# An encoder layer's embedding product moved from among the experts to a place ahead of the gates

## The chip, the cores and the metric

One Trainium2 chip, one core of it. The time is device microseconds of one execution of the whole program; lower is better. PE is the matrix engine, DVE the vector engine, ACT the scalar engine, POOL the general one, and SP issues most of the transfers (DMA). "PEclk" in a view is the clock that was granted to PE, as a share of full speed.

## The reference, cut to what matters

512 tokens of 1024 channels, two layers (`DEPTH = 2`), all in float32.

```python
for i in range(DEPTH):
    h = rmsnorm(x, norm_mix[i])
    proj = h @ w_in[i]
    na_q, na_k, na_v, q_lat, kv_lat, k_rope, gate_a, gate_b = jnp.split(proj, IN_CUTS, axis=-1)
    y_a = neighbourhood_attention(na_q, na_k, na_v, na_rpb[i]) @ w_na_o[i]      # 8 heads, window 8 x 16
    y_b = latent_attention(q_lat, kv_lat, k_rope, ...) @ w_mla_o[i]              # 8 heads
    merged = jax.nn.sigmoid(gate_a) * y_a + jax.nn.sigmoid(gate_b) * y_b
    x = x + merged @ w_out[i]
    x = x + expert_choice_moe(rmsnorm(x, norm_moe[i]), ...)   # 16 experts of 64 tokens each, FF 1024
    ple_gate = jax.nn.sigmoid(rmsnorm(x, norm_ple[i]) @ ple_gate_w[i])
    x = x + ple_gate * (p[i] @ ple_w[i])                      # p: 512 x 256, ple_w: 256 x 1024
return rmsnorm(x, norm_final)
```

The product `p[i] @ ple_w[i]` needs nothing that the layer computes. It is used only at the layer's end.

## The kernel before

All is written in one function, `trunk`, in program order; a scheduler then fixes the order of the instructions on each engine when the program is built, and on the chip each engine keeps to that order and waits where an operand or a buffer isn't ready. A tile of a pool is a buffer: the scheduler makes the next user of the same memory wait until the last user of the old tile is done, and pools that are opened on one side of the memory lie on top of one another like a stack, so a pool opened after another was closed lies on the memory of the closed one.

A layer has these stages:

- **Projections and latent attention.** Weights come through `load_w`: one transfer into `raw` (2 buffers), a copy `wh` on ACT and a rest `wl` on DVE (3 buffers each). A product in higher precision (`mm3`) is three PE products: high by high, high by low, low by high.
- **Neighbourhood attention** (L450 to L487). 8 heads of 4 column blocks, so 32 units a layer. A unit runs through the engines in turn: scores `s` on PE (two products, L462 and L463; 2 buffers in PSUM), bias and maximum on DVE (`sb`, L466; 3 buffers), exponential on ACT (L469), reciprocal on DVE (L471), scaling into one of four padded tiles `pad0` to `pad3` on POOL (L473), two or three transposes `tp` on PE (L477; 2 buffers), a copy `pt` on DVE or ACT (L479). Each two heads end with eight products `o` on PE (L485) and `put_y` on ACT and DVE.
- **Gates and branch outputs** (L494 to L521). For both branches and four column groups: two gate products `tp_` of 24 PE products each (`t_proj`) and two output products `op` of 12 each; the gates' sigmoids go to tiles `sg` of the pool `mp`. That is 8 times 72 products.
- **Output projection** `xo`, norm and router.
- **Experts.** Experts 0 to 3 are gathered one by one (`gather_one`) and computed whole; experts 4 to 9 are gathered together (`gather`, "gather A"), experts 10 to 15 too ("gather B", `GATHER_B = 7`). `hidden` makes the two first products `t` of an expert, whose weights come in tiles of 1 MiB (`w_tile`) into a ring of 15 slots of the pool `s8` (tag `s8`), so long as a slot is free. The outputs of experts 0 to 3 wait in one slot (`obs`) until `scatter` adds them to x, after `hidden` of expert 7. After `hidden` of expert 11 (`PLE_AT = 11`) stands the embedding's product `pw`: `load_s` takes six slots of the ring for p and the weights, 48 PE products follow through one PSUM buffer, and ACT copies the result to two tiles `pw` of a pool of its own.
- **Second products of experts 4 to 15** (`po`, L900), scatter (`sca`), the embedding's gate `pg`, and the end of the layer, where `pw` is used (L968).

Of the kernel before, what the change touches and what calls it, by code (L numbers as in the profile page):

```python
# [10 lines left out]
F32 = mybir.dt.float32  # L11
# [8 lines left out]
P = 128  # L20
D = 1024
S = 512
# [6 lines left out]
RING = 15  # L29
BLOCKED = 4  # L30
EARLY_END = ONE * 8 + BLOCKED * 4 - 4
GATHER_B = 7

PLE_AT = 11
SPL = 3
GTB = 1
S0B = 2
# [26 lines left out]
def trunk(ctx, tc, a, out, L=2, dbg=None):  # L64
# [12 lines left out]
    def slot(dt=F32, shape=(P, 4, S)):  # L77
        return s8.tile(list(shape), dt, tag="s8", name="s8")
# [15 lines left out]
    def acopy(o, i, scale=1.0):  # L94
        sc.activation(o, i, AF.Copy, scale=scale)  # L95
# [48 lines left out]
    def mm3(ps, pairs):  # L144

        n = 3 * len(pairs)
        i = 0
        for (sh, sl), (mh, ml) in pairs:
            for s_, m_ in ((sh, mh), (sh, ml), (sl, mh)):
                pe.matmul(ps, s_, m_, start=(i == 0), stop=(i == n - 1))  # L150
                i += 1
# [30 lines left out]
    for l in range(L):  # L182
# [258 lines left out]
        for c, ps in enumerate(wide([a["w_v"][l, i] for i in range(4)], hT_h, hT_l, "vp")[0]):  # L441
            acopy(v[:, c, :], ps)
        ya_h, ya_l = slot(F32R), slot(F32R)
        mt = ExitStack()
        mp = mt.enter_context(tc.tile_pool(name=f"m{l}", bufs=3, side="right", reuse_waits="tile"))
        with tc.tile_pool(name=f"na{l}", bufs=2, side="right", reuse_waits="tile") as ap_:
            pad = [ap_.tile([P, NCH[c] * P], F32, tag=f"pad{c}", bufs=1, name=f"pad{c}") for c in range(4)]
            for b in pad:
# [40 lines left out]
        if dbg and l == 0:  # L489
            dma(dbg["ya"].rearrange("(k p) t -> p k t", p=P), ya_h.bitcast(F32))  # L490


        tb = [slot() for _ in range(2)]
        m_h = [slot(F32R) for _ in range(2)]  # L494
# [81 lines left out]
                    nw[1] = d  # L576
            return t

        before = [kp.tile([P, 2, S], BF16, tag="row", bufs=3, name="before") for _ in range(2)]
        for i in range(2):  # L580
            sc.dma_start(before[i], a["before"][:, 2 * i:2 * i + 2, :])
        s4_ = small.tile([P, 4], F32, tag="s4_", name="s4_")
# [69 lines left out]
            pe.transpose(aT[:NE, c * P:(c + 1) * P], aff[:, c, :], ident)  # L652

        def row():
            return kp.tile([NE, S], F32, tag="row", bufs=3, name="row")


        cur = row()
# [1 line left out]
        for _ in range(CAP // 8):  # L660
# [2 lines left out]
            nxt = row()  # L663
            ve.match_replace(nxt, m8, cur, -1.0)
            cur = nxt
        sel = row()
        ve.tensor_scalar(sel, cur, 0.0, None, ALU.is_lt)
        cs = row()
        ve.tensor_tensor_scan(cs, sel, sel, 0.0, ALU.add, ALU.max)
        ps1 = row()  # L670
        ve.tensor_tensor(ps1.rearrange("e (c r) -> e r c", r=GH), cs.rearrange("e (r c) -> e r c", r=GH),
                         sel.rearrange("e (r c) -> e r c", r=GH), ALU.mult)
        pT = psT.tile([P, 4, NE], F32, tag="T", name="pT")
# [28 lines left out]
                ve.tensor_scalar(val[r, :], ps[r, ee:ee + 1], 0.5, None, ALU.mult)  # L702
            return svT, val

        def gather(pool, e0, n):

            xg = pool.tile([P, 8, n * CAP], F32, tag="xg", bufs=1, name="xg")
            s = ga.tile([P, 4, n, CAP], F32R, tag="sel", bufs=1, name="sel")
            for c in range(4):
                ve.tensor_tensor(s[:, c], bc(pos[:, c, e0:e0 + n], CAP), iota.unsqueeze(1).to_broadcast([P, n, CAP]), ALU.is_equal)  # L710
            for k in range(8):
                xh = ga.tile([P, 4, P], F32R, tag="xh", name="xh")
                xl = ga.tile([P, 4, P], F32R, tag="xl", name="xl")
                for c in range(4):
                    xv = x[:, c, k * P:(k + 1) * P]
                    sc.activation(xh[:, c, :], xv, AF.Identity, scale=rx[:, c:c + 1])
                    ve.scalar_tensor_tensor(xl[:, c, :], xv, rx[:, c:c + 1], xh[:, c, :].bitcast(F32), ALU.mult, ALU.subtract)
                ps = psS.tile([P, n * CAP], F32, tag="S", name="gat")
                for i in range(8):
                    pe.matmul(ps, (xh if i % 2 == 0 else xl)[:, i // 2, :], s[:, i // 2].rearrange("p a b -> p (a b)"),  # L720
                              start=(i == 0), stop=(i == 7))
                if k % 2:
                    sc.activation(xg[:, k, :], ps, AF.Identity, scale=g_moe[:, k:k + 1])
                else:
                    ve.tensor_scalar(xg[:, k, :], ps, g_moe[:, k:k + 1], None, ALU.mult)
            return xg

        def hidden(e, xg, new=None, between=None):


            t13 = []
            for wsrc in (a["moe_w1"], a["moe_w3"]):
                ps = psA.tile([P, S], F32, tag="A", name="t13")
                for k in range(8):
                    if k % 2 == 0:
                        w = w_tile(wsrc[l, e, k // 2])
                    for hf in range(2):
                        products.append(pe.matmul(ps[hf * 64:(hf + 1) * 64, :], xg(k), w[:, k % 2, hf * S:(hf + 1) * S],  # L738
                                                  start=(k == 0), stop=(k == 7)))
                    if between and k == 3 and not t13:  # L740
                        between()
                t13.append(ps)
            u = ep.tile([P, S], F32, tag="u", bufs=1, name="u")
            sc.activation(u, t13[0], AF.Tanh, scale=0.5)  # L744
            ve.scalar_tensor_tensor(u, u, 1.0, t13[0], ALU.add, ALU.mult)  # L745
            ve.tensor_tensor(u, u, t13[1], ALU.mult)  # L746

            def turn():
                last = products[-1]
                tp = psT.tile([P, 4, 2, CAP], F32, tag="T", name="gT")  # L750
                with tc.issue_after(last.ins):
                    for q in range(4):
                        pe.transpose(tp[:, q].rearrange("p a b -> p (a b)"), u[:, q * P:(q + 1) * P], ident)  # L753
                gT = new() if new else ep.tile([P, 4, 2, CAP], F32, tag="gT", bufs=GTB, name="gT")
                acopy(gT, tp)
                return gT

            return turn
# [13 lines left out]
        def scatter(pr, ob):  # L772

            svT, val = where(pr)
            for hf in range(2):
                oh = qp.tile([P, S], F32R, tag="oh", bufs=OHB, name="oh")
                ol = qp.tile([P, S], F32R, tag="oh", bufs=OHB, name="ol")
                o = ob[:, hf * S:(hf + 1) * S]
                sc.activation(oh, o, AF.Identity, scale=val)
                ve.scalar_tensor_tensor(ol, o, val, oh.bitcast(F32), ALU.mult, ALU.subtract)  # L780
                for c in range(4):
                    ps = psS.tile([P, S], F32, tag="S", name="sca")
                    pe.matmul(ps, svT[:, c * P:(c + 1) * P], oh, start=True, stop=False)
                    pe.matmul(ps, svT[:, c * P:(c + 1) * P], ol, start=False, stop=True)
                    xv = x[:, c, hf * S:(hf + 1) * S]
                    ve.tensor_tensor(xv, ps, xv, ALU.add)
# [14 lines left out]
                room.extend(t[:, i] for i in range(4))  # L801
            return room.pop(0)

        gTs, pw = [], []

        for e in range(ONE):
            gT = hidden(e, xg)()
# [9 lines left out]
                gt = ExitStack()  # L817
                ga = gt.enter_context(tc.tile_pool(name=f"ga{l}", bufs=2, reuse_waits="tile"))
            down(e, gT, obs[e // 2])
        xgA = gather(ga, ONE, NA_)  # L820
        rt.close()
        st, xt_, pt_ = ExitStack(), ExitStack(), ExitStack()

        def load_s(src, k=4):

            raw, h = slot(), slot(F32R)
            lo = slot(F32R) if k == 4 else h[:, k:2 * k, :]
            dma(raw[:, 0:k, :], src)
            for i in range(0, k, 2):
                acopy(h[:, i:i + 2, :], raw[:, i:i + 2, :])  # L830
                ve.tensor_sub(lo[:, i:i + 2, :], raw[:, i:i + 2, :], h[:, i:i + 2, :].bitcast(F32))
            return h, lo

        turn = None
        for e in range(ONE, NE):
            if e == GATHER_B:
                xgB = gather(xt_.enter_context(tc.tile_pool(name=f"x{l}", bufs=1, side="right", reuse_waits="tile")), ONE + NA_, NE - ONE - NA_)
            if e == ONE + NA_:
                gt.close()
                pp = pt_.enter_context(tc.tile_pool(name=f"ple{l}", bufs=2, reuse_waits="tile"))  # L840
            i = (e - ONE) % NA_
            xg = xgA if e < ONE + NA_ else xgB
            turn = hidden(e, lambda k: xg[:, k, i * CAP:(i + 1) * CAP], kept, turn and (lambda turn=turn: gTs.append(turn())))
            if e == GATHER_B:
                for pr in range(BLOCKED // 2):
                    scatter(pr, obs[pr])
            if e == PLE_AT:

                pT_ = load_s(a["p"][l], 2)
                for hf in range(2):  # L850
                    w = load_s(a["ple_w"][l, hf], 2)
                    pw.append(pp.tile([P, 4, S], F32, tag="pw", name="pw"))
                    for c in range(4):
                        ps = psO.tile([P, S], F32, tag="O", name="pw")
                        cs_ = slice(c * P, (c + 1) * P)
                        mm3(ps, [((pT_[0][:, k, cs_], pT_[1][:, k, cs_]), (w[0][:, k, :], w[1][:, k, :])) for k in range(2)])
                        acopy(pw[hf][:, c, :], ps, 0.5)
        gTs.append(turn())
        xt_.close()

# [119 lines left out]
                normed.append(norm_in(c, np_, grow, hh, hl))  # L980
        nt.close()
        st.close()
        pt_.close()
        qt.close()
        et.close()
# [126 lines left out]
```

## Time and profile before

| | us |
|---|---|
| median of 3 runs | 1950.42 |
| the three runs | 1944.68, 1950.42, 1953.80 |
| profiled execution, its own time | 1943.66 |
| its span in the profile | 1941.9 |
| PE busy, share of the span | 1876.7 (97%) |
| DVE busy | 782.3 (40%) |
| ACT busy | 593.0 (31%) |
| moved by DMA | 486.60 MB |

The two layers read alike in the trace; the second runs some 961 us behind the first (its gate stage ends at 1335.10 us, that of the first at 374.20). PE's busy time counts a product until its modelled end, so a stretch in which PE waits a little before each product can still read as fully busy; how long a stretch lasts and how many products it holds says more.

### The profile page before, as it was taken

To read this page: it belongs to the slowest core of one execution; us is meant where nothing else is said; L and a number is where in the kernel's file an instruction comes from. 1 tells how busy PE (TensorE), PEld (TensorE's weight loads), DVE (VectorE), ACT (ScalarE), POOL (GpSimd) and SP (SyncE) were. 2 spreads that over 40 slices of the span, in tenths; PEclk is the share of its full clock that TensorE was granted. 3 is DMA by queue.
4 is the path that set the end of the run, shared out by engine and by line. 5 is a ranking of instruction groups with operands and counts; after the bars stand their busy time and mean duration, and the time that the engine had idled before them with its cause. 6 is when DMAs were issued, how large, how long until landed. Compare 5 with 4: busy or idle time off the path is not lost.

```text
span 1941.9 us, 25362 instructions
## 1 busy us (share of the span) xinstructions
PE 1876.7 (97%) x10028; PEld 1195.3 (62%) x10028; DVE 782.3 (40%) x1662; ACT 593.0 (31%) x1219; POOL 84.3 (4%) x156
## 2 busy tenths in 40 slices
PE   7999999999999999999899999999999999999995
PEld 7776777883354333666687677788734533336664
DVE  4656353444233310323756554444442422112346
ACT  4646443320132110221436454423101410212222
POOL 0022110000000000000000221100000000000000
PEclk9999999999999999999999999999999999999998
DMA  5220323488989999977412103236799899999781
GB/s 165 66 76 23 111 77 108 180 347 334 395 358 379 427 426 427 426 309 311 157 44 76 47 25 119 78 106 239 298 396 385 346 400 427 426 426 379 303 335 66
DMA packets 80997, 486.60 MB, mean 251 GB/s; under 512 B 9200, under 2 KB 11760, under 8 KB 30448
## 3 DMA queue, kind: packets, MB, share of 16 engines
q1 hardware_dynamic: 78000, 478.71, 62.3%
q10 hardware_dynamic: 2880, 6.29, 1.0%
q8 instruction: 79, 1.29, 0.3%
q14 instruction: 38, 0.31, 0.0%
HBM read 482.87 MB, written 2.10 MB: 250 GB/s over the span
## 4 chain that ended last, share of the span: by engine, by line
PE 88%; DVE 5%; DMA 4%; ACT 2%; issue 1%; SPq 0%; DVEq 0%; ACTq 0%
PE t L738 19%; PE po L900 9%; PE op L150 5%; PE xo L241 5%; PE pg L150 4%; DMA w<-in_moe_w_dram 3%; PE po L766 3%; PE sca L915 3%; PE gat L720 2%; PE vp L241 2%; PE o L430 2%; PE tokp L150 2%; PE gat L636 2%; PE pw L150 1%; PE s L410 1%; PE tp L423 1%
## 5 line engine op out<-in xcount | busy, mean ns | idle before, releaser
L738 PE MATMUL t<-w,xg 128*64 128x512 f32 x2048 | 459.2, 597 | 3.9 <-DMA w<-in_moe_w_dram 2.2
L738 PEld LDWEIGHTS t<-w,xg 128*64 128x64 f32 x2048 | 141.6, 137 | 279.9 <-issue 263.6
L192 DVE TENSOR_TENSOR wl<-raw,wh 128x1024 fp32r<-128x1024 f32 (+2 forms) x110 | 127.7, 1161 | 158.5 <-ACT wh L95 157.8
L900 PE MATMUL po<-s,s 128*64 128x256 f32 x1536 | 190.0, 385 | 0.0
L900 PEld LDWEIGHTS po<-s,s 128*64 128x64 f32 x1536 | 109.4, 138 | 60.5 <-issue 7.9
L95 ACT ACTIVATE wh<-raw 128x1024 fp32r<-128x1024 f32 (+2 forms) x110 | 110.8, 1007 | 116.9 <-PE xo L241 30.8
L150 PE MATMUL pg<-s,hp 128*128 128x512 f32 x384 | 101.3, 406 | 1.1 <-ACT hp L95 1.1
L745 DVE SCALAR_TENSOR_TENSOR u<-u,t 128x512 f32<-128x512 f32 x32 | 22.0, 687 | 189.6 <-ACT u L744 189.5
L746 DVE TENSOR_TENSOR u<-u,t 128x512 f32<-128x512 f32 x32 | 21.9, 685 | 161.6 <-PE t L738 161.6
L150 PEld LDWEIGHTS pg<-s,hp 128*128 128x128 f32 x384 | 68.5, 188 | 24.7 <-issue 7.7
L241 PE MATMUL xo<-wh,s 128*128 128x512 f32 x256 | 80.8, 392 | 0.0
L150 PE MATMUL op<-s,wh 128*128 128x512 f32 x256 | 80.1, 392 | 0.0
L906 ACT ACTIVATE oh<-po,val 128x256 fp32r<-128x256 f32 x48 | 22.8, 475 | 170.0 <-PE po L900 169.5
L907 DVE SCALAR_TENSOR_TENSOR oh<-po,val,oh 128x256 fp32r<-128x256 f32 x48 | 23.2, 484 | 118.6 <-ACT oh L906 118.5
L95 ACT ACTIVATE s<-gT 128x512 f32<-128x512 f32 x24 | 14.3, 596 | 182.7 <-PE gT L753 182.7
L915 PEld LDWEIGHTS sca<-oh,svT 128*128 128x128 f32 x384 | 51.0, 189 | 16.0 <-issue 9.6
L915 PE MATMUL sca<-oh,svT 128*128 128x256 f32 x384 | 59.5, 292 | 0.3 <-ACT oh L906 0.2
L766 PE MATMUL po<-w,gT 128*64 128x512 f32 x256 | 59.5, 602 | 0.0
L417 ACT ACTIVATE p<-s,nm 128x512 f32<-128x512 f32 x64 | 43.9, 686 | 50.1 <-DVE nm L414 47.7
L420 POOL TENSOR_SCALAR p<-p,rs 128x512 f32<-128x512 f32 x64 | 44.4, 696 | 338.4 <-DVE rs L419 310.1
L414 DVE TENSOR_REDUCE nm<-s 128x1 f32<-128x512 f32 x64 | 44.2, 690 | 33.4 <-PE s L410 23.7
L744 ACT ACTIVATE u<-t 128x512 f32<-128x512 f32 x32 | 19.1, 598 | 124.6 <-PE t L738 124.6
(478 smaller groups left out, 3217.2 us busy)
## 6 DMA issues: line engine op xcount, KB each, us to landing
w<-in_moe_w_dram SPq DMA_DIRECT2D x288, 1024.0 KB, 11.1
s<-in_moe_w_dram SPq DMA_DIRECT2D x96, 1024.0 KB, 10.9
raw<-in_w_in_dram SPq DMA_DIRECT2D x48, 512.0 KB, 3.5
raw<-in_w_out_dram SPq DMA_DIRECT2D x16, 512.0 KB, 3.5
s<-in_ple_gate_w_dram SPq DMA_DIRECT2D x8, 1024.0 KB, 10.2
bias<-in_bias_dram ACTq DMA_DIRECT2D x16, 320.0 KB, 2.9
raw<-in_w_v_dram SPq DMA_DIRECT2D x8, 512.0 KB, 3.5
raw<-in_w_mla_o_dram SPq DMA_DIRECT2D x8, 512.0 KB, 3.5
```

Source lines behind the costliest of these rows:

```text
L95: sc.activation(o, i, AF.Copy, scale=scale)
L150: pe.matmul(ps, s_, m_, start=(i == 0), stop=(i == n - 1))
L192: ve.tensor_sub(wl, raw, wh.bitcast(F32))
L241: pe.matmul(ps[c], s_[2 * i + k][:, cs_], m_[:, k, :], start=(i + k + j == 0), stop=(i == 3 and k == 1 and j == 2))
L414: ve.tensor_reduce(nm, s, AX.X, ALU.max, negate=True)
L417: sc.activation(pr_, s, AF.Exp, bias=nm, accum_out=sm)
L420: gp.tensor_scalar(pr_, pr_, rs, 1.0, ALU.mult, ALU.mult)
L430: pe.matmul(o[hh_ * 64:(hh_ + 1) * 64, :], vm[:, j, h * 64:(h + 1) * 64], pts[hh_][:, j, :], start=(j == 0), stop=(j == 3))
L738: products.append(pe.matmul(ps[hf * 64:(hf + 1) * 64, :], xg(k), w[:, k % 2, hf * S:(hf + 1) * S], start=(k == 0), stop=(k == 7)))
L766: pe.matmul(po[hf * 64:(hf + 1) * 64, :], gT[:, k % 4, k // 4, :], w[:, k % 2, hf * S:(hf + 1) * S], start=(k == 0), stop=(k == 7))
L900: pe.matmul(po[ee * CAP:(ee + 1) * CAP, :], gTs[2 * n + ee][:, k % 4, k // 4, :], ws[ee][:, k, :], start=(k == 0), stop=(k == 7))
L915: pe.matmul(ps[:, j, :], sT[:, (c + j) * P:(c + j + 1) * P], o, start=(i == 0), stop=(i == len(parts) - 1))
```

## The change

Three things are moved, and one buffer is saved.

1. The embedding's product `pw` stands ahead of the gates in program order, behind the neighbourhood attention. Its operands come through `load_w` (the pool of the weights), its PSUM tiles from `psA` (3 buffers) and its results lie in a new pool `em`, which is opened after the pool of the neighbourhood attention (`na`) was closed, and stays until the layer's end. The gates' pool `m` (tiles `sg`) is opened on top of it; before, it was opened ahead of the pool `na`, below it.
2. Gather B is a generator of eight steps, of which `hidden` of experts 8 and 9 calls four each. Its order on PE relative to the products `t` around it comes out as before (its rows stand among those of expert 5 in both).
3. `scatter` of the first experts comes ahead of expert 12 rather than behind expert 7.
4. The tiles `row` of the router have 2 buffers, not 3, and the last of them, `ps1`, lies in the buffer of `u`.

```diff
-GATHER_B = 7
-
-PLE_AT = 11
+GATHER_B = 8
+
+SCATTER = 12
...
         ya_h, ya_l = slot(F32R), slot(F32R)
-        mt = ExitStack()
-        mp = mt.enter_context(tc.tile_pool(name=f"m{l}", bufs=3, side="right", reuse_waits="tile"))
         with tc.tile_pool(name=f"na{l}", bufs=2, side="right", reuse_waits="tile") as ap_:
...
+        et_ = ExitStack()
+        ew = et_.enter_context(tc.tile_pool(name=f"em{l}", bufs=2, side="right", reuse_waits="tile"))
+        pw = [ew.tile([P, 4, S], F32, tag="pw", name="pw") for _ in range(2)]
+        pT_ = load_w(a["p"][l], 2, S)
+        for hf in range(2):
+            w = load_w(a["ple_w"][l, hf], 2, S)
+            for c in range(4):
+                ps = psA.tile([P, S], F32, tag="A", name="pw")
+                cs_ = slice(c * P, (c + 1) * P)
+                mm3(ps, [((pT_[0][:, k, cs_], pT_[1][:, k, cs_]), (w[0][:, k, :], w[1][:, k, :])) for k in range(2)])
+                acopy(pw[hf][:, c, :], ps, 0.5)
+
+        mt = ExitStack()
+        mp = mt.enter_context(tc.tile_pool(name=f"m{l}", bufs=3, side="right", reuse_waits="tile"))
...
-        sel = row()
+        sel, cs = cur, row()
         ve.tensor_scalar(sel, cur, 0.0, None, ALU.is_lt)
-        cs = row()
         ve.tensor_tensor_scan(cs, sel, sel, 0.0, ALU.add, ALU.max)
-        ps1 = row()
+        ps1 = ep.tile([P, S], F32, tag="u", bufs=1, name="ps1")[:NE, :]
...
+                yield
...
+                    if steps and k % 4 == 3:
+                        next(steps, None)
...
         for e in range(ONE, NE):
+            if e == SCATTER:
+                for pr in range(BLOCKED // 2):
+                    scatter(pr, obs[pr])
             if e == GATHER_B:
...
-            if e == GATHER_B:
-                for pr in range(BLOCKED // 2):
-                    scatter(pr, obs[pr])
-            if e == PLE_AT:
-
-                pT_ = load_s(a["p"][l], 2)
-                for hf in range(2):
-                    w = load_s(a["ple_w"][l, hf], 2)
-                    pw.append(pp.tile([P, 4, S], F32, tag="pw", name="pw"))
-                    for c in range(4):
-                        ps = psO.tile([P, S], F32, tag="O", name="pw")
-                        cs_ = slice(c * P, (c + 1) * P)
-                        mm3(ps, [((pT_[0][:, k, cs_], pT_[1][:, k, cs_]), (w[0][:, k, :], w[1][:, k, :])) for k in range(2)])
-                        acopy(pw[hf][:, c, :], ps, 0.5)
```

On PE, in the neighbourhood attention of the first layer (second head), eleven rows in succession before. `tp__` is a gate product, `op` an output product of the latent branch, `s` are scores, `tp` transposes, `o` the attention's product:

```order
L477 MATMUL tp_2095<-ident_78,pad3_2029 128x128 x2
L485 MATMUL o_2164<-pt_2036,s8_1889 64x256
L150 MATMUL tp__2644<-s8_86,wh_2613 128x512
L150 MATMUL tp__2644<-s8_84,wl_2614 128x512
L150 MATMUL op_2677<-s8_1083,wh_2673 128x512
L150 MATMUL op_2677<-s8_1084,wh_2673 128x512
L462 MATMUL s_2133<-s8_568,s8_567 128x256
L463 MATMUL s_2133<-s8_569,s8_567 128x256
L150 MATMUL op_2677<-s8_1083,wl_2674 128x512
L462 MATMUL s_2149<-s8_568,s8_567 128x192
L463 MATMUL s_2149<-s8_569,s8_567 128x192
```

The same place of PE's order now (the lines of the file are two less here):

```order
L460 MATMUL s_2099<-s8_568,s8_567 128x192
L461 MATMUL s_2099<-s8_569,s8_567 128x192
L460 MATMUL s_2114<-s8_568,s8_567 128x256
L461 MATMUL s_2114<-s8_569,s8_567 128x256
L460 MATMUL s_2130<-s8_568,s8_567 128x256
L461 MATMUL s_2130<-s8_569,s8_567 128x256
L483 MATMUL o_2161<-pt_2033,s8_1889 64x256
L475 MATMUL tp_2076<-ident_78,pad2_2025 128x128 x3
L460 MATMUL s_2146<-s8_568,s8_567 128x192
L461 MATMUL s_2146<-s8_569,s8_567 128x192
L475 MATMUL tp_2092<-ident_78,pad3_2026 128x128 x2
```

No gate and no output product stands among the attention's rows any more: three `pw` products of 6 rows each do, near its start; the other five and all 576 products of the gate stage come behind its last `o`. Before, 288 of the 576 stood inside.

On ACT, at the end of that attention now: the last exponential, the last copies of transposes, the last `put_y` (`s8_2018`), and then the copies of `pw`:

```order
L467 ACTIVATE sb_2572,sm_2575<-sb_2572,nm_2573 128x192
L95 ACTIVATE pt_2521<-tp_2548 128x3x128
L95 ACTIVATE pt_2521<-tp_2580 128x2x128
L95 ACTIVATE s8_2018<-o_2584 128x512
L95 ACTIVATE pw_2599<-pw_2613 128x512
L95 ACTIVATE pw_2599<-pw_2621 128x512
L95 ACTIVATE pw_2599<-pw_2629 128x512
L594 DMA before_3903<-in_before_dram 128x1024
L594 DMA before_3904<-in_before_dram 128x1024
L95 ACTIVATE pw_2599<-pw_2637 128x512
```

The three `pw` products that are made early keep the three buffers of `psA` until here, since the tile that they are copied to lies on the memory of the attention's `pad` and `bias` tiles; the fourth (`pw_2637`) is made after the first copy.

On PE, where the first layer's expert 11 ended and expert 12 began before (`t13` are the products `t`, `gT` transposes of a hidden result):

```order
L738 MATMUL t13_5327<-w_5346,xg_4765 64x512 x4
L150 MATMUL pw_5367<-s8_5362,s8_5357 128x512 x6
L150 MATMUL pw_5375<-s8_5362,s8_5357 128x512 x6
L738 MATMUL t13_5437<-w_5438,xg_4765 64x512 x4
L150 MATMUL pw_5383<-s8_5362,s8_5357 128x512 x6
L738 MATMUL t13_5437<-w_5444,xg_4765 64x512 x4
L753 MATMUL gT_5450<-ident_78,u_5352 128x128 x4
L738 MATMUL t13_5437<-w_5456,xg_4765 64x512 x4
L150 MATMUL pw_5391<-s8_5362,s8_5357 128x512 x6
```

And in expert 11 now (`sca` are the scatter's products, which stood among those of experts 7 and 8 before):

```order
L770 MATMUL gT_5275<-ident_78,u_5258 128x128 x4
L705 MATMUL tp_5327<-ident_78,sv_5322 128x128 x4
L753 MATMUL t13_5262<-w_5281,xg_4911 64x512 x4
L710 MATMUL val_5334<-aff_3923,sv_5322 128x2 x4
L753 MATMUL t13_5262<-w_5287,xg_4911 64x512 x4
L800 MATMUL sca_5346<-oh_5342,svT_5332 128x512
L800 MATMUL sca_5350<-oh_5342,svT_5332 128x512
L801 MATMUL sca_5346<-ol_5343,svT_5332 128x512
L801 MATMUL sca_5350<-ol_5343,svT_5332 128x512
L800 MATMUL sca_5354<-oh_5342,svT_5332 128x512
```

The 48 products of `pw`, which ran on into expert 13, are gone from here, and 32 products of the scatter with their transposes stand among those of experts 11 and 12.

## Rows read from the trace of the kernel before

**Rows 1.** The page's busy times: us, share of the span, instructions.

```profile
PE 1876.7 (97%) x10028; PEld 1195.3 (62%) x10028; DVE 782.3 (40%) x1662; ACT 593.0 (31%) x1219; POOL 84.3 (4%) x156
```

**Rows 2.** Stretches of the first layer: busy us of each engine, PEclk, DMA, GB/s.

```profile
171.12:190.42 19.30, 19.13 (x120) 12.91 (x118) 12.75 (x28) 13.24 (x32) 6.22 (x9) 1.00 0.01 1
212.51:308.61 96.10, 96.10 (x495) 73.84 (x493) 44.54 (x133) 42.89 (x103) 14.05 (x31) 1.00 0.31 97
543.00:600.00 57.00, 57.00 (x274) 30.42 (x275) 23.61 (x67) 22.21 (x64) 0.00 (x0) 1.00 0.86 338
600.00:778.00 178.00, 173.53 (x782) 64.73 (x778) 33.92 (x63) 23.71 (x37) 0.00 (x0) 0.98 1.01 424
700.00:710.00 10.00, 6.68 (x18) 3.32 (x20) 4.09 (x4) 1.39 (x3) 0.00 (x0) 0.70 1.01 424
```

**Rows 3.** The chain that ended last, gate stage: start us, us, what.

```profile
308.68 5.68 PE tp__3017 L150 x24
...
336.12 5.44 PE op L150 x24
```

**Rows 4.** Groups by line and shape in 212.51 to 308.61: busy us, mean ns.

```profile
L192 DVE TENSOR_TENSOR wl<-raw,wh 128x1024 fp32r<-128x1024 f32 x13 | 15.9, 1223 | 9.1 <-ACT wh L95 9.0
...
L95 ACT ACTIVATE wh<-raw 128x1024 fp32r<-128x1024 f32 x13 | 13.8, 1059 | 12.9 <-PE op L150 7.8 <-PE tp__2944 L150 2.5 <-PE tp__2844 L150 1.1
...
L469 ACT ACTIVATE sb<-sb,nm 128x256 f32<-128x256 f32 x16 | 8.1, 504 | 9.8 <-DVE nm L466 9.8
...
L469 ACT ACTIVATE sb<-sb,nm 128x192 f32<-128x192 f32 x15 | 6.8, 452 | 7.4 <-DVE nm L466 7.3
L466 DVE CUSTOM_DVE_ANT_0 sb<-s,bias 128x256 f32<-128x256 f32 x16 | 6.8, 422 | 9.6 <-PE s L463 9.6
...
L466 DVE CUSTOM_DVE_ANT_0 sb<-s,bias 128x192 f32<-128x192 f32 x15 | 5.3, 353 | 11.3 <-PE s L463 9.3 <-issue 2.0
...
L471 DVE RECIPROCAL rs<-sm 128x1 f32<-128x1 f32 x31 | 4.9, 160 | 7.7 <-ACT sb L469 7.7
...
L479 DVE COPY pt<-tp 128x384 f32<-128x384 f32 x8 | 4.4, 548 | 2.6 <-PE tp L477 2.4
...
L95 ACT ACTIVATE pt<-tp 128x384 f32<-128x384 f32 x8 | 3.9, 491 | 4.7 <-PE tp L477 4.7
L479 DVE COPY pt<-tp 128x256 f32<-128x256 f32 x8 | 3.4, 423 | 7.2 <-PE tp L477 7.2
L95 ACT ACTIVATE pt<-tp 128x256 f32<-128x256 f32 x8 | 3.1, 382 | 9.6 <-PE tp L477 9.6
```

**Rows 5.** Timeline of one unit of the attention, scores to padded tile.

```profile
256.51 0.39 PE L462 MATMUL s<-s,s 128*128 128x256 f32 x1
...
257.16 0.42 DVE L466 CUSTOM_DVE_ANT_0 sb<-s,bias 128x256 f32<-128x256 f32 x1 [0.79 <-PE s L463]
...
257.63 0.51 ACT L469 ACTIVATE sb<-sb,nm 128x256 f32<-128x256 f32 x1 [1.21 <-DVE nm L466]
...
258.59 0.88 POOL L473 TENSOR_SCALAR pad<-sb,rs 128x256 f32<-128x256 f32 x2 [5.41 <-DVE rs L471]
```

**Rows 6.** The chain that ended last, expert stage: start us, us, what.

```profile
688.99 11.60 DMA w<-in_moe_w_dram
...
705.37 2.93 PE pw L150 x6
...
738.69 13.88 PE t L738 x64
...
758.35 19.56 DMA w<-in_moe_w_dram
```

**Rows 7.** DMA issues: count, KB each, median us to landing.

```profile
w<-in_moe_w_dram SPq DMA_DIRECT2D x288, 1024.0 KB, 11.1
...
s<-in_ple_w_dram SPq DMA_DIRECT2D x4, 512.0 KB, 14.7
...
s<-in_p_dram SPq DMA_DIRECT2D x2, 512.0 KB, 18.0
```

More of the change, by code (lines that the diff above doesn't have):

```diff
@@ L577, in w_tile @@
             return t
-        before = [kp.tile([P, 2, S], BF16, tag="row", bufs=3, name="before") for _ in range(2)]
+        before = [kp.tile([P, 2, S], BF16, tag="row", bufs=2, name="before") for _ in range(2)]
         for i in range(2):
@@ L654, in row @@
         def row():
-            return kp.tile([NE, S], F32, tag="row", bufs=3, name="row")
+            return kp.tile([NE, S], F32, tag="row", bufs=2, name="row")
         cur = row()
@@ L703, in where, with gather @@
             return svT, val
-        def gather(pool, e0, n):
-            xg = pool.tile([P, 8, n * CAP], F32, tag="xg", bufs=1, name="xg")
+        def gather(xg, e0, n):
             s = ga.tile([P, 4, n, CAP], F32R, tag="sel", bufs=1, name="sel")
@@ L725, in gather, with gathered, hidden @@
                     ve.tensor_scalar(xg[:, k, :], ps, g_moe[:, k:k + 1], None, ALU.mult)
-            return xg
-        def hidden(e, xg, new=None, between=None):
+                yield
+        def gathered(pool, n):
+            return pool.tile([P, 8, n * CAP], F32, tag="xg", bufs=1, name="xg")
+        def hidden(e, xg, new=None, between=None, steps=None):
             t13 = []
@@ L802, in kept @@
             return room.pop(0)
-        gTs, pw = [], []
+        gTs = []
         for e in range(ONE):
@@ L819, in trunk @@
             down(e, gT, obs[e // 2])
-        xgA = gather(ga, ONE, NA_)
+        xgA, steps = gathered(ga, NA_), None
+        for _ in gather(xgA, ONE, NA_):
+            pass
         rt.close()
         st, xt_, pt_ = ExitStack(), ExitStack(), ExitStack()
[L824 to L832, printed above, removed]
         turn = None
         for e in range(ONE, NE):
+            if e == SCATTER:
+                for pr in range(BLOCKED // 2):
+                    scatter(pr, obs[pr])
             if e == GATHER_B:
-                xgB = gather(xt_.enter_context(tc.tile_pool(name=f"x{l}", bufs=1, side="right", reuse_waits="tile")), ONE + NA_, NE - ONE - NA_)
+                xgB = gathered(xt_.enter_context(tc.tile_pool(name=f"x{l}", bufs=1, side="right", reuse_waits="tile")), NE - ONE - NA_)
+                steps = gather(xgB, ONE + NA_, NE - ONE - NA_)
             if e == ONE + NA_:
@@ L842, in trunk @@
             xg = xgA if e < ONE + NA_ else xgB
-            turn = hidden(e, lambda k: xg[:, k, i * CAP:(i + 1) * CAP], kept, turn and (lambda turn=turn: gTs.append(turn())))
-            if e == GATHER_B:
-                for pr in range(BLOCKED // 2):
-                    scatter(pr, obs[pr])
-            if e == PLE_AT:
-                pT_ = load_s(a["p"][l], 2)
-                for hf in range(2):
-                    w = load_s(a["ple_w"][l, hf], 2)
-                    pw.append(pp.tile([P, 4, S], F32, tag="pw", name="pw"))
-                    for c in range(4):
-                        ps = psO.tile([P, S], F32, tag="O", name="pw")
-                        cs_ = slice(c * P, (c + 1) * P)
-                        mm3(ps, [((pT_[0][:, k, cs_], pT_[1][:, k, cs_]), (w[0][:, k, :], w[1][:, k, :])) for k in range(2)])
-                        acopy(pw[hf][:, c, :], ps, 0.5)
+            turn = hidden(e, lambda k: xg[:, k, i * CAP:(i + 1) * CAP], kept, turn and (lambda turn=turn: gTs.append(turn())), steps)
         gTs.append(turn())
@@ L982, in trunk @@
         st.close()
+        et_.close()
         pt_.close()
```

## The prediction

> **What bounds the kernel now.** First the page's busy times [rows 1]: PE is busy for 97% of the span, DVE for 40%, ACT for 31%. That points at PE, but it is a mean over stages, so I next read stretches of the first layer, the two stages that the change touches [rows 2]. The reader is to compare three columns: PE's time, its instructions, and the share of DMA.
>
> In the attention's stretch (212.51 to 308.61, from the first gate product to the first one behind the attention) PE has no gap in 96.10 us and DMA stands at 0.31: PE bounds it. Gate products fill what the attention leaves. In the stretch 600 to 778 DMA stands at 1.01, with 424 GB/s moved: there the weights' transfers bound the kernel, whatever PE does. The chain of waits says the same [rows 6]: it goes through 11.60 us of a weight transfer from 688.99, and again through 19.56 us from 758.35. An expert's two first products take PE 13.88 us [rows 6], while their eight tiles of 1 MiB [rows 7], 8.39 MB, take 19.8 us at 424 GB/s. So each of these experts leaves PE some 5.9 us to spare, and other work in that stretch costs the kernel nothing. Ahead of it, in gather A (543 to 600), DMA is at 0.86: PE bounds again, and the ring is full. That part and all behind 778 are not touched by the change.
>
> So the change takes work out of a stretch where PE has time to spare and puts it into one where it has none, and by doing so takes the gates' products out from between the attention's.
>
> **The change part by part, for one layer.**
>
> *What the attention costs PE.* A fp32r product of 512 columns takes 5.44/24 = 0.2267 us [rows 3]. The stretch of 96.10 us holds 288 gate and output products (counted in the order), 65.3 us. The remaining 30.8 us are the attention's own products, 31 of its 32 units: 0.99 us a unit.
>
> *What the attention takes alone.* Now nothing but three `pw` products stands among its rows, so PE waits wherever the attention waits. How long is it then? No row shows this attention alone, so I bound it. From below: PE's own 30.8 us, plus 18 `pw` products, 4.1 us, plus about 1 us until the last copy: 36. DVE and ACT have nearly as much to do: DVE 24.8 us in the rows shown, ACT 21.9 [rows 4], and to both come the short instructions that read out a maximum or a sum, and `put_y`. Three engines about equally loaded, each in a fixed order, with every unit passing PE, DVE, ACT, DVE, POOL, PE and then DVE or ACT, can't all be kept full. A unit needs 258.59 − 256.51 = 2.08 us from its scores to the scaling, 0.44 us for the scaling [rows 5] and about 0.7 us for transposes and copy: some 3.5 us with handovers. The order puts scores four units ahead of the transposes, so this delay by itself allows 0.9 us a unit. But scores have two buffers, so that the third of three scores in a row waits for DVE. I walked one pair of heads, eight units, down the new order with these durations, starting each row when its operand, its buffer and its engine were ready: the same rows of the next pair come 8.1 to 8.7 us later, of which PE works 7.9. That is 1.05 us a unit. From above, the nearest row is the latent attention's stretch with hardly any other work [rows 2]: PE busy for 19.13 of 19.30 us, so such a chain of the same engines can leave PE nearly full; for the upper end I allow 1.4 us a unit, 40% over PE's own pace. I take 1.05, near the floor, because that row shows hardly a gap. The stretch then lasts 31 × 1.05 = 32.6, plus 4.1 for the three `pw` (the attention's rows queue behind them on PE), plus some 5 for the last unit's way to its last `o`: **42 us**, bounds 36 and 52.5 (43.4 + 4.1 + 5).
>
> *Behind it.* The first `pw` copy waits for `put_y`; with two passes over 512 columns, an estimated 0.6 us each from 0.49 for 384 [rows 4], and handovers PE stands some 1.6 us ahead of the fourth `pw`. Then come 30 `pw` products, 6.8 us, and the 288 deferred ones, 65.3 us. The first gate's weights wait for buffers that `pw` holds: cast and rest take 1.06 and 1.22 us [rows 4], 2.5 with handovers, beside 24 and then 23 products of 5.3 us, so they are covered; uncovered they would cost those 2.5 us twice.
>
> *The sum here*: 42 + 1.6 + 6.8 + 65.3 − 96.1 = +19.6 us.
>
> *What the expert stage gets back.* PE's 10.9 us of `pw`, its 3.3 us without work and the lower clock in 700 to 710 [rows 2] all lie inside the stretch that transfers bound, so they give nothing by themselves. What counts is the bytes: three tiles of 512 KB [rows 7], 1.57 MB, are 3.7 us at 424 GB/s. At the new place DMA has room (0.31). **−3.7 us**; from below 0, if a later wait eats them.
>
> *The scatter later*: 32 products (7.3 us) and some transposes move from experts 7 and 8 to experts 11 and 12, both ahead of 778, where two experts have nearly 12 us to spare; without that cover they would cost their 8 or 9 us. One slot of the ring stays taken for longer, while six are no longer taken by `load_s`. SP issues fewer transfers there, not more. Nothing. *Gather B in steps*: same order; nothing. *Two buffers for `row`, `ps1` in `u`*: each row of the router's search depends on the one before anyhow; expert 0's tanh must now wait for `ps1`'s transposes, and PE's order has the next gather in between. About 1 us a layer either way, left out.
>
> *Sum*: +19.6 − 3.7 = +15.9 a layer, +31.8 for two, against the profiled execution's own 1943.66 us: 1975.5. That execution lies 6.8 us under the median of the runs shown and 1.0 under the lowest, so I add half of the 6.8: **1979 us**. Bounds of the attention alone: 36 gives +9.9 a layer, 1963; 52.5 gives +26.4, 1996, or 2003 against the median.
>
> **The rule on PE's clock.** In the stretches of rows 2 the granted clock is 1.00, except for 0.70 in the 10 us in which PE stood for 3.3 us. The attention alone would leave PE with many waits, each well under 1 us by the walk, so the sum goes by the full clock. Beside it stands the Trainium skill, "TensorE: Matmul & The Clock Gate", section "A second HAM failure mode: psum-queue depth-cycling": a kernel that cycled through PSUM banks left PE idle for so short times between groups of products, and so often, that its clock went back and forth between its levels. By that rule the clock would fall here as well; the row of the latent attention (1.00 over 19.30 us) speaks against it. Its result is the second rival.
>
> **The rivals.**
>
> *The attention alone is slower than 1.4 us a unit.* For it: each engine's order was made for other durations than the chip's, and a wait on one engine holds all behind it. Against it: the latent attention's row. At 1.4 to 1.8 us: 52.5 to 65, 1996 to 2021 on the profile's base.
>
> *The clock halves in it.* PE's 34.9 us then take 69.8, and 69.8 − 42 = 27.8 us a layer come on top: 2031.
>
> *Not slower: the expert stage gives back all of `pw`.* The place is 700 to 738, where `pw` stands. If PE's lateness and not the transfers sets when expert 15 ends, taking `pw` out gives 10.9 + 3.3 us and some 2 us at the lower clock, 16 rather than 3.7. Then +3.6 a layer, +7.2: 1951 on the profile's base, no difference; were the attention alone at its floor of 36, −2.4 a layer, which still reads as no difference. It decides from 11 us a layer on. For it: the chain goes through PE between its two transfers, by `pw` at 705.37 [rows 6]. Against it: DMA at 1.01 over the whole stretch [rows 2], and the chain's next piece, 19.56 us, is a transfer behind others: 8.3 MB at 424 GB/s.
>
> *That the change doesn't do what it says*: the order shows that it does, but for gather B.
>
> **How the numbers follow.** A measurement of this kernel tells a change of about 0.5% (9.8 us) from none. Forecast (36 to 52.5 us): 0.70. Slower attention: 0.15. Halved clock: 0.06. Expert stage gives all back: 0.09, of which 0.03 faster, if yet more is freed there than worked out. So faster 0.03, same 0.06, slower 0.91. The range goes from the floor, 1963, to 2008, a little above the forecast's upper bound and into the first rival: outside lie the last two rivals (0.15) and the end of the first.
>
> **What would show it.** In the changed profile: attention rows without gate products, the time from the vector product's end to the last `o` at 42 us (36 to 52), PE idle or slow there, PEclk still 1.00; a short stop ahead of the fourth `pw`; the output projection some 20 us later in the first layer; then DMA at 1.01 as before and the span from the output projection to the layer's end shorter by 3 to 4 us. The prediction is wrong if the expert stage shrinks by over 10 us a layer, or if the attention alone is far from 42 us.

## The result, and the profile after

The changed kernel takes 1970.58 us (median of six runs, 1968.97 to 1972.74), the kernel before 1944.89 us beside it (six runs, 1938.13 to 1953.80): ratio 1.0126, interval 1.0107 to 1.0145. That is 25.7 us slower. The forecast was 1979 us, within 1963 to 2008. The profiled execution has a span of 1970.9 us, 29.0 above that of before.

The page's busy times after, to be laid beside [rows 1]:

```profile
PE 1882.2 (96%) x10028; PEld 1197.4 (61%) x10028; DVE 782.4 (40%) x1662; ACT 591.2 (30%) x1219; POOL 84.2 (4%) x156
```

PE does the same number of instructions, and its share of the span barely moves. Where the time went can't be read from this row; it needs stretches. Three windows of the first layer follow (columns as in [rows 2]): the attention (from the first `pw` product to the fourth), all behind it up to the output projection, and the stretch that transfers bound.

```profile
212.19:252.21 40.02, 36.97 (x224) 24.74 (x223) 24.82 (x114) 26.55 (x86) 13.93 (x31) 1.00 0.25 75
252.21:389.88 137.67, 137.67 (x607) 114.04 (x608) 51.41 (x56) 44.37 (x57) 0.00 (x0) 1.00 0.33 105
609.10:790.70 181.60, 168.74 (x763) 56.68 (x761) 30.62 (x60) 16.34 (x27) 0.00 (x0) 1.00 1.00 421
```

The attention alone holds PE for 40.02 us at the full clock and leaves it some 3 us idle; behind it PE has no gap at all until the output projection. In the last row PE has 12.9 us without work and DMA none. The chain of waits shows the same handover, in the gate stage of the first layer and then among the experts:

```profile
252.21 7.11 PE pw L150 x30
...
270.20 5.44 PE op L150 x24
...
389.88 23.80 PE xo L241 x105
...
638.67 16.23 DMA w<-in_moe_w_dram
654.96 19.50 DMA w<-in_moe_w_dram
674.54 19.54 DMA w<-in_moe_w_dram
...
729.92 19.55 DMA w<-in_moe_w_dram
749.54 19.56 DMA w<-in_moe_w_dram
769.16 19.56 DMA w<-in_moe_w_dram
```

Before, the gate stage ran from product to product from 308.68 on [rows 3] and the output projection began at 374.20; now it begins 15.7 us later. Among the experts the chain, which before went through `pw` at 705.37 between two transfers [rows 6], now goes from transfer to transfer.

How the time splits is best seen by landmarks in PE's order. All numbers of this table are worked out from starts and ends of PE's rows in the timeline, first layer / second layer: "attention and gates" from the last `vp` to the first `xo`; "norm" from there to the first `aT`; "first experts" to the last `gat`, which ends both gathers; "transfers' stretch" to the last `t`; "second products" from there to the last `po`. The first line is the kernel before, the others are differences to it in us.

| kernel | attention and gates | norm | first experts | transfers' stretch | second products |
|---|---|---|---|---|---|
| before | 161.6 / 161.6 | 68.4 / 68.4 | 152.4 / 152.1 | 185.0 / 184.7 | 166.0 / 166.4 |
| changed | +15.9 / +15.8 | 0.0 / +4.6 | −1.5 / +0.5 | −3.4 / −4.5 | −0.3 / +2.9 |
| changed, profiled again | +16.0 / +15.8 | 0.0 / 0.0 | −0.1 / −1.2 | −2.9 / −4.3 | −0.3 / +2.9 |
| gates behind | +4.6 / +4.7 | −0.1 / −0.1 | +1.1 / 0.0 | −0.9 / −0.3 | −0.3 / +1.4 |
| no `pw` transfers | 0.0 / 0.0 | 0.0 / 0.0 | −1.7 / +1.6 | −3.7 / −0.1 | +1.8 / −0.3 |
| no `pw` products | 0.0 / 0.0 | 0.0 / 0.0 | 0.0 / 0.0 | −0.1 / +0.1 | +2.1 / +3.5 |
| pools below | +10.7 / +10.7 | 0.0 / 0.0 | +0.1 / +0.5 | −3.3 / −3.2 | −0.3 / +2.8 |
| changed, without `pw` | +4.6 / +4.6 | 0.0 / 0.0 | +0.2 / +0.3 | −2.1 / −3.8 | +3.6 / −0.3 |
| rest of the change | 0.0 / 0.0 | +4.6 / 0.0 | +0.3 / +0.6 | 0.0 / +0.2 | +3.6 / +3.2 |
| `pw` in the router | 0.0 / 0.0 | +0.3 / +4.9 | +1.9 / +2.2 | −2.1 / −3.6 | −1.3 / +1.8 |
| `pw` spread | 0.0 / 0.0 | +1.0 / +1.0 | +1.8 / +2.2 | −3.3 / −4.5 | −1.3 / +1.8 |

The layer's end and the next projections (227.4 us before, once in the program) vary from −3.7 to +1.0 us among these kernels and stand in no column.

### The profile page after: what moved, and what is told of

Same layout as the page of the kernel before. It is cut to its first block, busy times and chain, and to the rows that moved or that the text cites. A ratio compares the mean times of both kernels' runs of the same rounds, so it can differ in the third digit from the quotient of the medians.

```text
span 1970.9 us, 25396 instructions
## 1 busy us (share of the span) xinstructions
PE 1882.2 (96%) x10028; PEld 1197.4 (61%) x10028; DVE 782.4 (40%) x1662; ACT 591.2 (30%) x1219; POOL 84.2 (4%) x156
## 4 chain that ended last, share of the span: by engine, by line
PE 81%; DMA 10%; DVE 5%; ACT 2%; issue 1%; POOL 0%; SPq 0%; ACTq 0%; DVEq 0%; POOLq 0%
PE t L753 14%; DMA w<-in_moe_w_dram 10%; PE po L899 9%; PE xo L241 4%; PE op L150 4%; PE pg L150 4%; PE po L783 3%; PE sca L914 3%; PE gat L731 2%; PE vp L241 2%; PE o L430 2%; PE tokp L150 2%; PE latp L150 2%; PE gat L649 1%; PE s L410 1%; PE tp L423 1%
## 5 line engine op out<-in xcount | busy, mean ns | idle before, releaser
L753 PE MATMUL t<-w,xg 128*64 128x512 f32 x2048 | 465.7, 597 | 23.9 <-DMA w<-in_moe_w_dram 23.6
L192 DVE TENSOR_TENSOR wl<-raw,wh 128x1024 fp32r<-128x1024 f32 (+2 forms) x116 | 135.1, 1165 | 218.3 <-ACT wh L95 217.1
L95 ACT ACTIVATE wh<-raw 128x1024 fp32r<-128x1024 f32 (+2 forms) x116 | 117.2, 1010 | 157.9 <-PE op L150 34.9
L150 PEld LDWEIGHTS pg<-s,hp 128*128 128x128 f32 x384 | 68.4, 188 | 25.8 <-issue 8.7
## 6 DMA issues: line engine op xcount, KB each, us to landing
s<-in_moe_w_dram SPq DMA_DIRECT2D x96, 1024.0 KB, 10.7
```

What stands on the lines that cost most here:

```text
L192: ve.tensor_sub(wl, raw, wh.bitcast(F32))
```

## The experiments

Theory A is the prediction's: a moved product costs what its new stretch has no room for, and gives back only its bytes where it came from. The rivals are that the lost overlap of gates and attention is the whole loss, or that PE's lateness sets the end of the expert stage.

**Gates behind.** The kernel before, with the gates' pool alone moved:

```diff
-        mt = ExitStack()
-        mp = mt.enter_context(tc.tile_pool(name=f"m{l}", bufs=3, ...))
         with tc.tile_pool(name=f"na{l}", ...) as ap_:
...
+        mt = ExitStack()
+        mp = mt.enter_context(tc.tile_pool(name=f"m{l}", bufs=3, ...))
         tb = [slot() for _ in range(2)]
```

> The kernel before with one thing moved: the pool of the gates' tiles is opened behind the attention's pool, as in the changed kernel; the embedding's product stays among the experts. In PE's order 60 gate and output products (13.6 us at 0.2267) are now left inside the attention instead of 288. Theory A: what this costs is only the time in which PE waits for the attention, no more than the 5.1 us that the changed kernel shows for 212.19 to 252.21 (40.0 us against 30.8 + 4.1 of work): the output projection starts 3 to 5 us later in a layer, 6 to 10 us in all, ratio 1.003 to 1.005. Rival: the lost overlap is what makes the changed kernel slower: about 16 us a layer, 1.016.

Measured: 1.0037 (1.0020 to 1.0054). The output projection, by the chain of waits:

```profile
373.41 5.44 PE op L150 x24
378.85 3.17 PE xo L241 x14
```

It starts at 378.85 rather than 374.20. The lost overlap by itself costs 4.6 us a layer, not 16; 60 of the 288 products are still inside the attention here.

**No `pw` transfers, no `pw` products.** Two kernels that each take one half of `pw` out of its old place:

```diff
-            dma(raw[:, 0:k, :], src)
+            gp.memset(raw[:, 0:k, :], 0.5)
```

> The kernel before, with the three 512 KB transfers of the embedding's operands left out in each layer (POOL fills the operands with a constant; the 48 products, the casts and the slots stay). Theory A: the transfers bound this stretch, so it gets 3.4 to 3.7 us shorter a layer, 7 us in all, ratio 0.9965. Rival: PE's lateness by the products sets the end of the stretch, so nothing changes, 1.000.

```diff
...
-                        mm3(ps, [...])
-                        acopy(pw[hf][:, c, :], ps, 0.5)
+                        acopy(pw[hf][:, c, :], (pT_ if c < 2 else w)[0][:, c % 2, :].bitcast(F32), 0.5)
```

> The kernel before, with the embedding's 48 products left out in each layer (the result tiles are copied from the operands; the transfers, casts, slots and copies stay). Theory A: PE has time to spare there, so nothing changes within 1 us a layer, 1.000. Rival: the products set the end of the stretch: 11 to 16 us a layer come back, 0.984 to 0.989.

Measured: without the transfers 0.9973 (0.9958 to 0.9987); without the products 1.0035 (1.0021 to 1.0049). The windows of both in the stretch that transfers bound (first both layers of the kernel without transfers; then the first layer of the kernel before; then that of the kernel without products):

```profile
593.80:775.10 181.30, 177.78 (x811) 65.88 (x809) 34.16 (x63) 24.28 (x38) 2.85 (x3) 1.00 1.00 421
1551.50:1736.20 184.70, 179.84 (x811) 66.07 (x809) 34.16 (x63) 24.28 (x38) 2.85 (x3) 0.99 1.00 415
```

```profile
594.90:779.90 185.00, 180.52 (x811) 66.98 (x809) 33.92 (x63) 24.29 (x38) 0.00 (x0) 0.98 1.00 420
```

```profile
595.20:780.10 184.90, 169.12 (x763) 56.60 (x761) 34.01 (x63) 23.78 (x38) 0.00 (x0) 1.00 1.01 421
```

Leaving out 48 products takes PE's busy time from 180.5 to 169.1 us, and the stretch lasts as long as before; leaving out 1.57 MB shortens it by 3.7 us in the first layer. In the second the transfers ran at 415 GB/s instead of 421, which over 184.7 us is 2.6 us, so that layer shows hardly a gain; why they ran slower is open, and 1 us of the expected 3.7 stays without an account. What the bytes are worth is thus seen in one layer of this pair. That the products are worth nothing there is seen in both (−0.1 and +0.1). The rival that PE's lateness sets the end has fallen. That the kernel without products is slower as a whole lies in its second products; more on that below.

**Pools below.** The changed kernel with both pools opened ahead of the attention's, and `sb` with two buffers to make room:

```diff
+        et_ = ExitStack()
+        ew = et_.enter_context(tc.tile_pool(name=f"em{l}", ...))
+        mt = ExitStack()
+        mp = mt.enter_context(tc.tile_pool(name=f"m{l}", ...))
         with tc.tile_pool(name=f"na{l}", ...) as ap_:
...
-                        sb = ap_.tile([P, 256], F32, tag="sb", bufs=3, name="sb")
+                        sb = ap_.tile([P, 256], F32, tag="sb", bufs=2, name="sb")
```

> The changed kernel with both pools, that of the embedding's result and that of the gates' tiles, opened ahead of the attention's pool and below it; to make room, the attention's score tiles sb have two buffers instead of three. In PE's order the embedding's product and then gate products fill the attention again. Theory A: what the changed kernel pays is mostly the embedding's own 10.9 us of products in a stretch that PE bounds; the waits go, so a layer stands 10.9 - 3.4 = 7.5 us above the kernel before, 15 us in all, ratio 1.008, and 10 to 12 us under the changed kernel. Rival: the lost overlap is the whole loss: the result is then no slower than the kernel before, 0.9965 to 1.000.

Measured: 1.0093 (1.0074 to 1.0112). The output projection starts at 384.59, with the attention filled again (the chain, then the window from the attention's start to the output projection, in which PE has no gap):

```profile
379.15 5.44 PE op L150 x24
384.59 5.44 PE xo L241 x24
```

```profile
212.13:384.40 172.27, 172.27 (x831) 137.19 (x830) 76.98 (x169) 71.15 (x141) 13.89 (x31) 1.00 0.31 101
```

So the overlap can be had back whole and the kernel still loses 10.7 us a layer ahead of the output projection: the time of the 48 products, 10.9 us.

**Changed, without `pw`.** The eight lines from `pT_ = load_w(...)` to the copy are replaced by `for t in pw: gp.memset(t, 0.5)`.

> The changed kernel with the embedding's product left out altogether (three transfers, casts, 48 products and eight copies a layer; POOL fills the two result tiles with a constant). Theory A: what the product costs at its new place is its own 10.9 us of PE, and the waits of the attention cost the 4.6 us a layer that the run with the gates behind the attention showed; so the output projection starts 4 to 5 us later than in the kernel before, some 11 us earlier than in the changed one, the expert stage stays 3.4 us shorter, and the total comes to +1 us a layer, ratio 1.000 to 1.003. Rival: the waits of the attention are the larger part, and the product hides in them: the output projection then starts 10 us or more later than before, ratio 1.006 or more.

Measured: 1.0026 (1.0012 to 1.0040). The output projection starts 4.6 us late in both layers, as with the gates behind. The product thus costs 15.9 − 4.6 = 11.3 us of the changed kernel's 15.9, the waits 4.6. Here too 60 gate and output products stand inside the attention, where the changed kernel has 18 of `pw`, so the split compares kernels that fill it differently; the 10.7 us of the pools below agree with it.

**Rest of the change.** The changed kernel with `pw` back at `PLE_AT = 11` and the gates' pool back ahead of the attention.

> The changed kernel with the embedding's product put back among the experts and the gates' pool back below the attention's: what is left of the change is the later scatter, the gather in steps, two buffers for row and ps1 in the buffer of u. Theory A (these were costed at nothing, 1 us a layer either way): 0.999 to 1.001. Rival: the scatter's products beside the embedding's own, both now in experts 11 and 12, overfill the time that the transfers leave: 3 us or more a layer slower, 1.003 or more.

Measured: 1.0017 (1.0007 to 1.0027). Not nothing, but not where the rival has it: the transfers' stretch stays within 0.2 us; the 3.6 and 3.2 us lie in the second products.

**`pw` in the router, and spread.** Products are put where PE waits for the router's chain on DVE, partly in place of warm-up products (`WARM`, products whose results nobody uses). The diff is that of the first version:

```diff
-WARM = (16, 8, 3)
+WARM = (0, 2, 3)
...
+        embed(1, m_lg)
...
+        embed(3, m)
...
+            if e == 0:
+                embed(4, products[-1])
```

> The changed kernel with the gates' pool back below the attention's, and the embedding's product put into the router's waits: its operands come at the end of the gate stage, six products stand in place of part of the warm-up products ahead of rowp, 18 in place of those behind it, 12 ahead of pT, where PE of the kernel before waits 2.7 us, and 12 behind pT. Theory A (a product costs what the stretch it stands in has no room for, and its bytes cost 3.4 us only where transfers bound): the first 36 cost nothing, the last 12 cost 2.7 us, the expert stage is 3.4 us shorter: about 1 us a layer faster than the kernel before, ratio 0.997 to 1.001. Rival: the product costs its 10.9 us wherever it stands outside the expert stage: 7.5 us a layer slower, 1.008.

Measured: 1.0008 (0.9993 to 1.0024).

> The kernel with the embedding's product in the router's waits, with its 48 products spread further: six in place of the warm-up products ahead of the last router products lg, six ahead of rowp, 18 behind it, 12 ahead of pT, and the last six behind the first products of expert 1 rather than 12 behind pT. Theory A (a product costs what its stretch has no room for): of the 12 that cost 2.7 us behind pT, six now cost some 0.5 us at the first place and six some 0.6 us behind expert 1, so a layer is 1.5 us shorter than in that kernel and about 2 us shorter than in the kernel before: ratio 0.997 to 0.999. Rival: the operands' six slots of the ring, held some 25 us longer, or the order of the later stages take it back: 1.000 or more.

Measured: 0.9994 (0.9983 to 1.0006), no difference. The transfers' stretch gives its 2.1 to 4.5 us, and the norm and the first experts take 2.2 to 3.2 us, the fall of clock below aside. `pw` thus costs 2 or 3 us here, 11 behind the attention, and some 4 by its bytes in its old place. The 1.5 us that the second version was to save didn't come: the six products in place of the last warm-ups cost 0.7 us more in the norm, and the first experts took as long as in the first version. No kernel tried that does the whole work is measurably faster than the one before.

**Changed, profiled again.**

> The changed kernel itself once more, unaltered. In its first profile the second layer took 73.0 us from the output projection's start to the transposes aT, against 68.5 in the kernel before and 68.4 in its own first layer, at a granted clock of 0.50 for some 9 us. If the clock's fall belonged to that one execution, this stretch takes 68.4 us now; if it is built into the change, 73 us again. Ratio to the kernel before: 1.0107 to 1.0145 either way.

Measured: 1.0122 (1.0105 to 1.0139), and 68.4 us for that stretch. The window of the first profile, then that of the second:

```profile
1360.40:1433.40 73.00, 71.80 (x396) 61.73 (x395) 27.80 (x59) 16.80 (x34) 0.00 (x0) 0.93 0.78 315
```

```profile
1363.30:1431.70 68.40, 67.16 (x395) 56.91 (x393) 27.79 (x59) 16.82 (x34) 0.00 (x0) 1.00 0.75 308
```

4.6 of the first profile's 29.0 us belonged to that one execution.

## Why the prediction was right, and which terms were off

**The direction and its reason** were right and are shown: PE's work went from a stretch in which transfers set the end into one in which PE does. What PE waited for in the first layer's transfers' stretch (us in total, times, longest), before and then after:

```profile
PE t L738 <- DMA w<-in_moe_w_dram: 1.1, 2, 0.6
```

```profile
PE t L753 <- DMA w<-in_moe_w_dram: 11.8, 23, 0.6
```

The products that were taken out left waits for weights of about their own length.

**What the attention takes alone** was mis-sized. The first `pw` starts at 212.26 and the last `o` ends at 251.04: 38.8 us, not 42; the stop ahead of the fourth `pw` is 1.2 us, not 1.6. Timeline of the attention's end (PE's rows; in brackets the idle time ahead):

```profile
244.79 0.27 PE L461 MATMUL s<-s,s 128*128 128x192 f32 x1
244.96 0.41 PE L475 MATMUL tp<-ident,pad 128*128 128x128 f32 x2
245.29 0.65 PE L483 MATMUL o<-pt,s 128*64 128x256 f32 x2
245.87 0.44 PE L475 MATMUL tp<-ident,pad 128*128 128x128 f32 x2
247.00 1.63 PE L475 MATMUL tp<-ident,pad 128*128 128x128 f32 x8 [0.69 <-POOL pad L471]
248.56 2.48 PE L483 MATMUL o<-pt,s 128*64 128x256 f32 x14
252.21 0.50 PE L150 MATMUL pw<-wh 128*128 128x512 f32 x1 [1.18 <-ACT pw L95]
```

The last scores end at 245.06, 32.8 us after the start, with the three `pw` inside. That is 28.7 us for 31 units, 0.93 each, where I had 1.05 and then added 5 us for the last unit's way. But in the 6.0 us behind the last scores PE waits only some 0.8 us, nearly all of it in the 0.69 ahead of the last transposes. The other 5.2 are PE's own transposes and `o`, which my 0.99 a unit [rows 2, 3] already contained: I counted them twice. With 38.8, 1.2, 7.1 for the 30 `pw` and 65.3 for the deferred gate products, less 96.1, the sum is +16.3; the table has +15.9. Of the forecast's +19.6, 10.9 were the product and 8.7 waits; the runs show 11.3 and 4.6. The walk's main claim held: three engines in a fixed order kept PE nearly full, 36.97 of 40.02 us.

**The clock** stayed at 1.00 over the attention alone, where PE stopped nine times, for 3.05 us in all and 1.18 at most; the rival of the halved clock has fallen. The Trainium skill ("TensorE: Matmul & The Clock Gate", section "A second HAM failure mode: psum-queue depth-cycling") tells of another kernel in which short stops between groups of products came so often that the clock went back and forth. The window 212.19 to 252.21 shows no such thing; a kernel with more frequent stops was not tried.

**The expert stage's −3.7 us** was right: −3.4 and −4.5 in one profile, −2.9 and −4.3 in the other. That it is not the products is shown by the kernel without them, in both layers. That it is the bytes is shown by the kernel without transfers in its first layer (−3.7) and hidden in its second by the slower transfers.

**"All behind 778 are not touched" was wrong.** I read it off the diff, but the scheduler orders each layer anew. In the second layer's second products four `sca` products stand 30 rows of `po` earlier than before, at two places, and PE waits for their operand `oh` at both, 1.5 us in the gaps that are shown as waits. The first place, by the timeline of the changed kernel:

```profile
1798.85 4.10 PE L899 MATMUL po<-s,s 128*64 128x256 f32 x34
1803.12 1.02 PE L914 MATMUL sca<-oh,svT 128*128 128x256 f32 x4 [0.17 <-ACT oh L905]
1804.08 3.67 PE L899 MATMUL po<-s,s 128*64 128x256 f32 x32
1808.31 1.98 PE L914 MATMUL sca<-oh,svT 128*128 128x256 f32 x12 [0.56 <-ACT oh L905]
```

and the same place of the kernel before, with no wait:

```profile
1772.88 7.13 PE L900 MATMUL po<-s,s 128*64 128x256 f32 x64
1779.93 0.74 PE L915 MATMUL sca<-oh,svT 128*128 128x256 f32 x4
1780.60 0.65 PE L900 MATMUL po<-s,s 128*64 128x256 f32 x2
1781.18 1.69 PE L915 MATMUL sca<-oh,svT 128*128 128x256 f32 x12
```

That is the +2.9 us, the same in both profiles and (+2.8) with the pools below, so it is built into the program. The kernel with the gates behind has one such place in its second layer instead of two, half of the waits (us in total, times, longest; the changed kernel first), and +1.4 us:

```profile
PE sca L914 <- ACT oh L905: 1.5, 4, 0.6
```

```profile
PE sca L915 <- ACT oh L906: 0.7, 2, 0.6
```

The same stage carries what slowed the kernel without `pw` products and the rest of the change; PE waits there for `oh` too, 1.3 and 2.0 us a layer, but that such waits are the whole of it was not tried apart.

One thing hides in the table's column of the second products. In its second layer the kernel before ran this stage with a short fall of PE's clock (0.57 over 1745.00 to 1749.00). With the same order of products and no fall, the first layer of `pw` in the router took 1.7 us less (the kernel before, then that layer):

```profile
1740.21:1906.63 166.42, 165.45 (x1189) 114.59 (x1189) 55.91 (x106) 37.57 (x82) 0.00 (x0) 0.99 0.79 322
```

```profile
780.05:944.76 164.71, 163.79 (x1189) 113.87 (x1189) 57.82 (x108) 39.34 (x84) 0.00 (x0) 1.00 0.83 339
```

The changed kernel has this fall in both profiles, and so have the gates behind, the pools below and the kernel without `pw` products. The other five kernels lack it in their second layer and read some 1.7 us too low there: −0.3 without transfers is one late place, 1.4, less 1.7.

**The later scatter, the gather in steps, the row buffers** cost nothing in the stages in which they stand (rest of the change: 0.0 to +0.6 us). What came with them is the later order: +3.6 us in the first layer, and +3.2 in the second, where the 1.7 us are missing.

**The sum.** Forecast +31.8 us; by the second profile +16.0 +15.8 −0.1 −1.2 −2.9 −4.3 −0.3 +2.9 = +25.9. The attention was 7.4 us too dear for two layers. The stages that the forecast put at nothing came to −1.3 (first experts) and +2.6 (second products); that they nearly cancel is luck. Of the 3.4 us for the base, 1.2 were due: the median of six runs of before lies that far above its profiled execution.

## What to carry to other kernels

Ask of a moved piece of work which resource sets the end of the stretch it leaves and of the one it enters: here 48 products and 1.57 MB were worth some 4 us where transfers bound, 11 us where PE did, and 2 to 3 in the router's waits. When working out what a chain takes alone, don't add the last unit's way on top of PE's total, since part of that way is PE work already counted. And where a scheduler orders the program, look at its order in every later stage, not only where the diff stands: four small products moved ahead of their operand, at two places, cost 2.9 us in a stage that the forecast took for untouched.

## What the runs showed of the hardware

The granted clock fell in single executions in the middle of a stretch that ran at full clock in others. In the first profile of the changed kernel, second layer, during the router's first products:

```profile
1413.00:1416.00 3.00, 3.00 (x18) 3.00 (x17) 1.42 (x7) 0.00 (x0) 0.00 (x0) 0.55 0.99 418
1416.00:1419.00 3.00, 3.00 (x16) 3.00 (x16) 0.53 (x3) 0.00 (x0) 0.00 (x0) 0.50 1.03 429
1419.00:1422.00 3.00, 3.00 (x16) 3.00 (x16) 0.93 (x5) 0.26 (x1) 0.00 (x0) 0.50 0.98 415
```

PE's rows ahead of it are the same as in the second profile, with the same wait of 0.51 us for `h`. The fall, to the lower of the clock's two levels, costs 4.6 us. At this place it came three times in the 22 layers profiled here: also in the first layer of the rest of the change (clock 0.93 over 73.0 us) and in the second of `pw` in the router (0.93 over 73.3 us), two kernels that were profiled once. What sets it off is open. A difference of 5 us between two single executions of this kernel therefore says little by itself; the landmarks by stage say where it lies.
